# A hybrid attention backbone on one core: the second layer's gate products placed between its attention steps

## The chip, the core and the metric

The kernel runs on one core of one Trainium2 chip, as one program. The metric is device time in microseconds (us). Before the change the median of three runs is 2137.03 us (2135.74 to 2137.96).

The core has a matrix engine (TensorE, PE), a vector engine (VectorE, DVE), a scalar engine (ScalarE, ACT), a general engine (GpSimd, POOL) and a queue that issues most transfers (SyncE, SP). Each takes its own instructions in the order in which the program lists them; semaphores hold an instruction back until what it needs is there. So an instruction that waits also holds all that stands behind it on its engine.

## The reference

Two layers work on 256 latent tokens x and 256 context tokens h, 1024 channels each. Cut to what matters here:

```python
for l in range(DEPTH):                       # DEPTH = 2
    x, h = x + ffn(...), h + ffn(...)        # half-step SwiGLU
    # mixing: u = modulated norm; one input projection gives all of these
    cq, ckv, kr, dq, dk, dv, pool_in, gates = split(u @ w_in)
    o_mla  = softmax_attention(q(rmsnorm(cq)), k(rmsnorm(ckv), kr), v(...))   # 8 heads
    o_diff = (softmax(q1 k1) - lam * softmax(q2 k2)) @ dv                     # 8 heads, rms norm per head
    o_pool = pool_proj(window_mean(pool_in) - pool_in)                        # 4 groups, windows 2/4/8/16
    g = sigmoid(gates + b_gate)                                               # 3 branches x 1024 channels
    merged = g[0]*(o_mla @ w_br_mla) + g[1]*(o_diff @ w_br_diff) + g[2]*(o_pool @ w_br_pool)
    x = x + mod * (merged @ w_out)           # h likewise, not in the last layer
    x = x + ffn(...)                         # h likewise, not in the last layer
return rmsnorm(x)
```

In the second layer only x is needed after the mixing, so queries, gates, branches and the output work on 256 columns, and only keys and values on all 512.

## The kernel before

**Products.** Activations lie as 128 channels by 512 tokens (latent in columns 0 to 255). Every product is done as three passes on fp32r data: high part times high part, and the two cross products with a low part (`mm3`, L305; the matmul itself is L310). A weight block of 128x128 against 256 tokens is thus three matmuls, and a product over 1024 input channels is 24.

**Weights.** They stream from memory as 406 chunks of 128x1024 float32 (512 KB), in the order in which the products ask for them (`Weights.take`). When a product opens chunk c, `pump` requests chunk c+3: SP loads it (`w`, L152), ACT casts its high part (`hi`, L153), and the low part (`lo`, L161) is a subtraction, on POOL in two halves of 128x512 while `on_pool` is true, otherwise on DVE in one 128x1024 instruction. There are four raw buffers and four of each part. The first 24 chunks of the second layer's mixing (271 to 294) were split earlier and lie in memory as two parts, so SP loads both and no engine works on them.

**Mixing.** It has 12 attention units in the second layer: eight of differential attention (0 to 7: four head pairs, two query blocks each), then four pairs of heads of latent attention (8 to 11). A unit is a score product into PSUM banks (L820, or L1148), a softmax (row maximum on DVE, exponential on ACT, L836 or L1170), norm steps (POOL and DVE; L1179 in the latent units), a transposition on PE (`tr`, L883) that ACT and DVE split into `pth` and `ptl`, and the product with the values (`po`, L906 to L909).

**The order between units** is written out by hand. SCHEDULE has one string for each layer, cut at `|` into rounds. Round 0 stands before the first unit, round n behind the scores and softmax of unit n-1, and rounds 13 to 18 in the merge below. A token is an item issued at that point: `dk1` to `dk3` and `dq1` to `dq3` the differential keys and queries, `kv`, `cq`, `kr` the latent inputs, `ls` their norms' statistics (its `rb` is the broadcast, L968, behind a reciprocal, L945), `k`, `q`, `v0`/`v1`, `ma` to `md` further keys, queries and values, `p0` to `p3` a pool group's product with its POOL work, `pp` the split of that (`pdh`, L349), `pj` its projection, `st`/`dn` the head norms, `om` the split of a latent output. `N` is the next norm step of the last unit, `T` the transposition of the oldest open unit, `V` its value product, `P` and `D` put `on_pool` to true and false.

**Gates.** `g<dm><b>` is one of the 24 gate products (output block dm 0 to 7, branch b: 0 latent, 1 differential, 2 pool), 24 matmuls each. One that stands in a round up to 12 is copied out of PSUM (L1303), written to memory (L1308) and fetched back (L1315) in the merge; one in round 13 or later is copied and stays in its page. Those that no round names are made in the merge loop, with the sigmoid straight from PSUM (L1396); the others take the sigmoid from their page (L1391).

**Merge.** For each dm, in the order b = 2, 1, 0: the gate (made or taken), then the branch product `br` (12 matmuls), then gate times branch on DVE (L1407). In dm = 0 a round is issued behind each gate and each branch. At dm = 1 `on_pool` becomes false.

Of the kernel before, what the change touches and what calls it, by code (L numbers as in the profile page):

```python
# [17 lines left out]
D = 1024  # L18
KD = 8
T = 512  # L20
# [35 lines left out]
)  # L56


# [1748 lines left out]
```

## Time and profile before

| | |
|---|---|
| median of three runs | 2137.03 us (2135.74 to 2137.96) |
| the profiled execution | 2135.98 us, span 2134.2 us |
| mean granted clock of PE | 0.997 |
| PE busy | 2110.2 us, 99% of the span |
| DVE, ACT, POOL busy | 61%, 42%, 41% |
| transfers | 409.21 MB, mean 192 GB/s |

The span is what the trace covers; the time of the execution has 1.8 us around it. Times in the rows are microseconds from the span's start. The second layer's attention lies at about 1640 to 1830, its merge at about 1830 to 1900.

### The profile page before, as it was taken

To read this page: it belongs to the slowest core of one execution; us is meant where nothing else is said; L and a number is where in the kernel's file an instruction comes from. 1 tells how busy PE (TensorE), PEld (TensorE's weight loads), DVE (VectorE), ACT (ScalarE), POOL (GpSimd) and SP (SyncE) were. 2 spreads that over 40 slices of the span, in tenths; PEclk is the share of its full clock that TensorE was granted. 3 is DMA by queue.
4 is the path that set the end of the run, shared out by engine and by line. 5 is a ranking of instruction groups with operands and counts; after the bars stand their busy time and mean duration, and the time that the engine had idled before them with its cause. 6 is when DMAs were issued, how large, how long until landed. Compare 5 with 4: busy or idle time off the path is not lost.

```text
span 2134.2 us, 31733 instructions
## 1 busy us (share of the span) xinstructions
PE 2110.2 (99%) x12068; PEld 1821.0 (85%) x12068; DVE 1297.5 (61%) x2008; ACT 899.4 (42%) x1530; POOL 883.5 (41%) x768
## 2 busy tenths in 40 slices
PE   9999999999999999999999999999999999999998
PEld 6888888977887788988888898888889888999998
DVE  7565655456656799457647644443444777567755
ACT  4433233345565533432212243332333557555544
POOL 0443435322475411567657754444353347401000
PEclk9999999999999999999999999999999999999999
DMA  7477777354322466245444526776674642455653
GB/s 286 178 295 278 252 265 281 106 207 138 114 94 74 150 235 237 99 158 180 167 166 162 178 95 226 286 286 237 250 263 153 225 163 99 166 198 192 232 182 116
DMA packets 119533, 409.21 MB, mean 192 GB/s; under 512 B 13266, under 2 KB 17234, under 8 KB 119380
## 3 DMA queue, kind: packets, MB, share of 16 engines
q1 hardware_dynamic: 103540, 354.74, 47.4%
q10 hardware_dynamic: 15840, 52.44, 6.2%
q8 instruction: 95, 1.56, 0.3%
q14 instruction: 58, 0.48, 0.1%
HBM read 348.80 MB, written 58.33 MB: 191 GB/s over the span
## 4 chain that ended last, share of the span: by engine, by line
PE 90%; ACT 4%; DVE 4%; issue 1%; POOL 1%; DMA 0%; ACTq 0%; DVEq 0%; POOLq 0%
PE dn L310 22%; PE fg L310 19%; PE fu L310 19%; PE gt L310 8%; PE it L310 7%; PE br L310 5%; PE vi L310 2%; ACT pe L836 1%; PE fg L1614 1%; PE fu L1614 1%; PE tr L883 1%; PE pa L1541 1%; PE sc L1148 1%; PE po L907 1%; ACT pe L1170 1%
## 5 line engine op out<-in xcount | busy, mean ns | idle before, releaser
L161 POOL TENSOR_TENSOR lo<-w,hi 128x512 fp32r<-128x512 f32 x410 | 644.7, 1597 | 583.2 <-ACT hi L153 552.7
L153 ACT CAST hi<-w 128x1024 fp32r<-128x1024 f32 x359 | 375.0, 1048 | 586.2 <-DMA w<-in_stream 227.6
L280 DVE CUSTOM_DVE_ANT_0 junk<-a,cvec 128x1024 bf16<-128x1024 f32 x224 | 350.6, 1565 | 3.7
L161 DVE TENSOR_TENSOR lo<-w,hi 128x1024 fp32r<-128x1024 f32 x154 | 188.8, 1232 | 139.7 <-ACT hi L153 139.6
L310 PE MATMUL dn<-hh,hi 128*128 128x512 f32 (+1 forms) x800 | 272.7, 341 | 0.0
L310 PE MATMUL dn<-hl,hi 128*128 128x512 f32 (+1 forms) x800 | 272.2, 340 | 0.0
L310 PE MATMUL dn<-hh,lo 128*128 128x512 f32 (+1 forms) x800 | 272.2, 340 | 0.0
L310 PE MATMUL fg<-uh,hi 128*128 128x512 f32 (+2 forms) x712 | 252.1, 354 | 0.0
L310 PE MATMUL fg<-ul,hi 128*128 128x512 f32 (+2 forms) x712 | 251.6, 353 | 0.0
L310 PE MATMUL fu<-ul,hi 128*128 128x512 f32 (+2 forms) x712 | 251.6, 353 | 0.0
L310 PE MATMUL fu<-uh,hi 128*128 128x512 f32 (+2 forms) x712 | 251.6, 353 | 0.0
L310 PE MATMUL fg<-uh,lo 128*128 128x512 f32 (+2 forms) x712 | 251.5, 353 | 0.0
L310 PE MATMUL fu<-uh,lo 128*128 128x512 f32 (+2 forms) x712 | 251.5, 353 | 0.0
L310 PEld LDWEIGHTS dn<-hl,hi 128*128 128x128 f32 x800 | 151.7, 190 | 17.0
L310 PEld LDWEIGHTS dn<-hh,hi 128*128 128x128 f32 x800 | 151.7, 190 | 17.0
L310 PEld LDWEIGHTS dn<-hh,lo 128*128 128x128 f32 x800 | 151.7, 190 | 16.7
L610 DVE TENSOR_TENSOR h<-sg,fu 128x512 f32<-128x512 f32 x66 | 45.2, 686 | 189.0 <-PE fu L310 110.8
L649 DVE SCALAR_TENSOR_TENSOR X<-dn,md,X 128x256 f32<-128x256 f32 x112 | 50.1, 479 | 173.0 <-PE dn L310 173.0
L310 PEld LDWEIGHTS fu<-uh,lo 128*128 128x128 f32 x712 | 134.5, 189 | 18.4
L310 PEld LDWEIGHTS fg<-ul,hi 128*128 128x128 f32 x712 | 134.6, 189 | 18.4
L310 PEld LDWEIGHTS fu<-uh,hi 128*128 128x128 f32 x712 | 134.6, 189 | 18.4
L310 PEld LDWEIGHTS fg<-uh,lo 128*128 128x128 f32 x712 | 134.5, 189 | 18.4
(322 smaller groups left out, 4367.4 us busy)
## 6 DMA issues: line engine op xcount, KB each, us to landing
w<-in_stream SPq DMA_DIRECT2D x359, 512.0 KB, 4.2
a<-in_ada SPq DMA_DIRECT2D x136, 512.0 KB, 4.6
el<-in_stream SPq DMA_DIRECT2D x47, 512.0 KB, 3.6
early<-eh ACTq DMA_DIRECT2D x47, 512.0 KB, 2.7
early<-el ACTq DMA_DIRECT2D x47, 512.0 KB, 3.7
hi<-early SPq DMA_DIRECT2D x47, 512.0 KB, 4.3
lo<-early SPq DMA_DIRECT2D x47, 512.0 KB, 5.3
a<-in_stream SPq DMA_DIRECT2D x8, 512.0 KB, 5.0
```

The lines of the kernel that those rows point to most:

```text
L153: copy(hi, raw)
L161: eng.tensor_tensor(out=lo[:, c], in0=raw[:, c], in1=hi[:, c].bitcast(F32), op=ALU.subtract)
L280: nc.vector.tensor_tensor_reduce(out=self.junk, in0=raw, in1=self.cvec[:, s, :], scale=1.0, scalar=0.0, op0=ALU.mult, op1=ALU.add, accum_o ...
L310: nc.tensor.matmul(out, a, b, start=first and n == 0, stop=last and n == 2)
L610: nc.vector.tensor_tensor(out=h[:, c], in0=sg[:, c], in1=pu[:, c], op=ALU.mult)
L649: nc.vector.scalar_tensor_tensor(out=x, in0=p[:, SC[s]], scalar=K.mod(self.l, m, s, dm), in1=x, op0=ALU.mult, op1=ALU.add)
L836: nc.scalar.activation(e[:, c], banks[i][:, c], AF.Exp, bias=nm[:, o:o + 1], scale=1.0, accum_out=ls[:, o:o + 1])
L883: nc.tensor.transpose(t[:, i * 128:i * 128 + 128], P[:, i * 128:i * 128 + 128], self.ident)
L907: nc.tensor.matmul(out[0:64], v[:, o:o + 64], lo[:, n, :], start=False, stop=False)
L1148: nc.tensor.matmul(out[qt], a[0:96, q0:q0 + 128], b[0:96, kc], start=n == 0, stop=n == 2)
L1170: nc.scalar.activation(e[:, o:o + nk], out[qt], AF.Exp, bias=nm[:, i:i + 1], scale=1.0, accum_out=ls[:, i:i + 1])
L1614: nc.tensor.matmul(b, w[n // 2], x, start=k == n == 0, stop=k == KD - 1 and n == 2)
```

## The change

Only the second string of SCHEDULE is another one. No instruction's shape changes and PE has the same matmuls.

```diff
-    "dk1 dq2 N | N P N N N dq1 cq0 kv0 | P N T kv1 N | N N | dk2 N N N N D N N dk3 N N T N N dq3 cq1 N N N V N "
-    "cq2 P N N N | N V g10 N N N N | N T N N ls T v0 nk0 nk1 V N kr N kc0 N nq0 kc1 nq1 | nq2 N v1 N N V P N kc2 "
-    "N | kc3 g20 N P T q1 V T N k0 q4 q0 q2 g41 T N V p3 V N k1 ma N | mb q3 T q5 k2 | N V sq T N p1 | g50 st N "
-    "ds1 V N mc N pp1 md N N N N N q6 N T N N q7 k3 pp3 N N pj1 p2 g12 | N T N ds0 N V om0 N pp2 | V dr1 N dn3 "
-    "p0 g11 dr0 dn1 om1 pj2 T pj3 N pp0 g00 om2 pj0 dn0 V | dn2 g01 N | | om3 N | N |",
+    "N dq3 N N dq1 | kv0 | dk1 N cq0 N dq2 N N N | T P N N V N P N N N D N dk2 N kv1 | P N T N dk3 N N N g40 N "
+    "cq1 N | N N T N cq2 N V N N N N | N N g10 ls v0 T V nk0 nk1 N kr N N N kc0 nq0 kc1 N nq1 P | nq2 N v1 N g20 "
+    "P N kc2 T N | kc3 V q1 N V q4 T q2 q0 k0 g31 T N N V p3 | ma T N k1 N g41 N k2 q3 q5 V mb g32 | | g02 N N V "
+    "sq N T N p1 g50 N st N V mc pp1 N md N N g71 N q6 T q7 k3 p2 pp3 N V ds1 pj1 N N ds0 g22 | N pp2 N | g51 "
+    "om0 g42 T g60 g12 dr1 dr0 g11 om1 p0 pj3 g72 pj2 V dn3 dn0 T N g52 pp0 g00 g70 pj0 g01 g61 g30 dn1 | g62 "
+    "dn2 V om2 | om3 N | N | N N N N N |",
```

Before, five gates are spilled (g10, g20, g41, g50, g12), three are made in rounds 13 and 14 and kept, and 16 are left to the merge loop. Now ten are spilled (g40, g10, g20, g31, g41, g32, g02, g50, g71, g22), 13 are kept from rounds 13 and 14, and one, g21, is left to the loop. So five more gates stand ahead of the last unit, and ten more stand behind it in the first rounds of the merge. Counted over the program, 14 chunks' low parts move from DVE to POOL (410 to 438 halves on POOL, 154 to 140 on DVE), SP gets five more spills and five more fetches of 128 KB, ACT 15 more copies, and 15 sigmoids read a page instead of PSUM.

The first place is the ACT engine around unit 9, the second pair of latent heads. `qf<-it` is the copy of a query product out of PSUM, `qh` the cast of a finished query, `kh` a key, `mv` a value, `pe,ls<-sc,nm` the exponentials of a unit. Before:

```order
L1170 ACTIVATE pe,ls<-sc,nm 128x512 x4
L349 CAST mv<-vi 128x4x64 x2
L153 CAST hi_15772<-w_15774 128x1024
L1109 COPY qf<-it 64x256
L349 CAST pth<-tr 128x4x128 x2
L1109 COPY qf<-it 64x256
L352 ACTIVATE qh_15794<-qf 96x256
L349 CAST kh<-it 64x512 x2
L352 ACTIVATE qh_15826<-qf 96x256
L1170 ACTIVATE pe,ls<-sc,nm 128x512 x4
```

And now:

```order
L1171 ACTIVATE pe,ls<-sc,nm 128x512 x4
L350 CAST mv<-vi 128x4x64 x2
L350 CAST pth<-tr 128x4x128 x2
L350 CAST kh<-it 64x512 x2
L1304 COPY sg<-gt 128x256
L350 CAST kh<-it 64x512 x2
L1110 COPY qf<-it 64x256 x2
L353 ACTIVATE qh_15864<-qf 96x256
L350 CAST mv<-vi 128x4x64 x2
L154 CAST hi_15905<-w_15907 128x1024
L154 CAST hi_15912<-w_15914 128x1024
L353 ACTIVATE qh_15882<-qf 96x256
```

The two query copies now stand next to each other, behind a gate's copy and a second pair of keys, and values and weight casts stand between the finished queries. Behind this piece the exponentials of units 9 and 10 follow each other.

The second place is the POOL engine, where the last pool group's work (`pp`, `pw`, `po`, `ed`) stands among the weights' low parts. Before:

```order
L161 TENSOR_TENSOR lo_16316<-w_16317,hi_16315 128x512 x2
L1179 TENSOR_SCALAR pe<-pe,ri 128x512 x4
L161 TENSOR_TENSOR lo_16457<-w_16458,hi_16456 128x512 x2
L161 TENSOR_TENSOR lo_16521<-w_16522,hi_16520 128x512 x2
L1021 MEMSET pp 128x8
L1022 MEMSET pp 128x8
L1031 TENSOR_TENSOR pw<-pp 128x271
L1038 TENSOR_SCALAR po_16542<-pw 128x256
L1040 TENSOR_TENSOR po_16542<-po_16542,pp 128x256
```

And now:

```order
L162 TENSOR_TENSOR lo_16519<-w_16520,hi_16518 128x512 x2
L1180 TENSOR_SCALAR pe<-pe,ri 128x512 x4
L162 TENSOR_TENSOR lo_16602<-w_16603,hi_16601 128x512 x2
L162 TENSOR_TENSOR lo_16640<-w_16641,hi_16639 128x512 x2
L162 TENSOR_TENSOR lo_16706<-w_16707,hi_16705 128x512 x2
L162 TENSOR_TENSOR lo_16740<-w_16741,hi_16739 128x512 x2
L162 TENSOR_TENSOR lo_16778<-w_16779,hi_16777 128x512 x2
L162 TENSOR_TENSOR lo_16816<-w_16817,hi_16815 128x512 x2
L1022 MEMSET pp 128x8
L1023 MEMSET pp 128x8
L1032 TENSOR_TENSOR pw<-pp 128x271
L1039 TENSOR_SCALAR po_16837<-pw 128x256
```

Between the last unit's norm (`pe<-pe,ri`) and the last pool group stood the low parts of two chunks, now those of six.

The third place is ACT where that pool group is split (`pdh<-po`) for its projection `pj0`. Before:

```order
L349 CAST pth<-tr 128x4x128 x4
L349 CAST oph_16649<-pf 128x256
L349 CAST pdh<-po_16542 128x256
L153 CAST hi_16661<-w_16663 128x1024
L1303 COPY sg<-gt 128x256
L349 CAST omh_16691<-om_14335 128x256
L349 CAST oph_16701<-pf 128x256
```

And now:

```order
L350 CAST pth<-tr 128x4x128 x4
L154 CAST hi_16974<-w_16976 128x1024
L1304 COPY sg<-gt 128x256
L350 CAST pdh<-po_16837 128x256
L154 CAST hi_17012<-w_17014 128x1024
L1304 COPY sg<-gt 128x256
L154 CAST hi_17046<-w_17048 128x1024
L1304 COPY sg<-gt 128x256
L350 CAST oph_17082<-pf 128x256
```

A gate's copy now stands ahead of the split and two behind it before the projection's result (`oph`), where only one stood behind it.

## Rows read from the trace of the kernel before

**Rows 1.** Windows: stretch, length; busy PE, PEld, DVE, ACT, POOL; PEclk, DMA share, GB/s

```profile
1600.00:1700.00 100.00, 98.28 (x729) 89.50 (x729) 56.79 (x123) 42.21 (x101) 33.72 (x41) 1.00 0.55 190
1700.00:1800.00 100.00, 94.02 (x666) 82.54 (x665) 73.52 (x132) 63.11 (x145) 50.83 (x69) 0.98 0.36 123
1800.00:1830.00 30.00, 27.64 (x199) 25.19 (x198) 19.53 (x34) 20.73 (x44) 24.66 (x34) 0.94 0.49 163
...
1870.00:1910.00 40.00, 40.00 (x335) 40.00 (x335) 24.62 (x34) 20.50 (x31) 3.01 (x4) 1.00 0.61 203
```

**Rows 2.** Waits of PE, 1500 to 1960: total us, times, longest us

```profile
PE sc L1148 <- ACT qh L352: 3.8, 1, 3.8
PE it L310 <- ACT pdh L349: 2.1, 1, 2.1
PE rb L968 <- DVE r L945: 1.4, 1, 1.4
PE it L310 <- ACT pe L836: 1.3, 1, 1.3
PE it L310 <- ACT pe L1170: 0.7, 1, 0.7
PE it L310 <- DMA lo<-early: 0.3, 1, 0.3
```

**Rows 3.** Timeline of PE at unit 9: start, us, instruction [idle before <- releaser]

```profile
1754.47 0.28 PE L310 MATMUL it<-cqh,lo 128*128 128x256 f32 x1
...
1760.29 0.39 PE L1148 MATMUL sc<-kh,ql 96*128 96x512 f32 x1
1764.46 0.69 PE L1148 MATMUL sc<-kh,qh 96*128 96x512 f32 x1 [3.77 <-ACT qh L352]
```

**Rows 4.** Timeline of ACT at the same place

```profile
1760.49 0.36 ACT L1109 COPY qf<-it 64x256 f32<-64x256 f32 x1
...
1763.99 0.42 ACT L352 ACTIVATE qh<-qf 96x256 fp32r<-96x256 f32 x1 [1.90 <-POOL qf L1113]
```

**Rows 5.** Timeline of DVE ahead of the broadcast of the latent norms

```profile
1706.92 3.34 DVE L945 RECIPROCAL r<-r 2x512 f32<-2x512 f32 x1
```

**Rows 6.** Timeline of PE at the last pool group's projection

```profile
1819.39 0.28 PE L310 MATMUL gt<-uh,hi 128*128 128x256 f32 x1
...
1822.15 0.28 PE L310 MATMUL gt<-uh,lo 128*128 128x256 f32 x1
1824.53 0.39 PE L310 MATMUL it<-pdh,hi 128*128 128x256 f32 x1 [2.09 <-ACT pdh L349]
```

**Rows 7.** Timeline of POOL at the last pool group

```profile
1813.02 5.22 POOL L161 TENSOR_TENSOR lo<-w,hi 128x512 fp32r<-128x512 f32 x4
...
1820.82 0.19 POOL L1048 TENSOR_TENSOR po<-ed,pp 128x1 f32<-128x1 f32 x1
```

**Rows 8.** Line L161 in 1735 to 1850: duration ns min/median/max, first and last start

```profile
L161 POOL TENSOR_TENSOR lo<-w,hi x30: 1262/1293/1502, 1750.9 to 1838.8; 128x512 fp32r<-128x512 f32 x30
```

**Rows 9.** The page, part 5: groups of the whole program (busy us, mean ns | idle before)

```profile
L161 POOL TENSOR_TENSOR lo<-w,hi 128x512 fp32r<-128x512 f32 x410 | 644.7, 1597 | 583.2 <-ACT hi L153 552.7
L153 ACT CAST hi<-w 128x1024 fp32r<-128x1024 f32 x359 | 375.0, 1048 | 586.2 <-DMA w<-in_stream 227.6
...
L161 DVE TENSOR_TENSOR lo<-w,hi 128x1024 fp32r<-128x1024 f32 x154 | 188.8, 1232 | 139.7 <-ACT hi L153 139.6
```

**Rows 10.** Transfers issued in 1735 to 1850: KB each, median us to landing

```profile
w<-in_stream SPq DMA_DIRECT2D x22, 512.0 KB, 3.9
...
sg<-g SPq DMA_DIRECT2D x4, 128.0 KB, 2.2
```

**Rows 11.** Lines by form, 1735 to 1850: busy us, mean ns | idle before

```profile
L1179 POOL TENSOR_SCALAR pe<-pe,ri 128x512 f32<-128x512 f32 x16 | 11.1, 716 | 5.6 <-DVE ri L1177 4.0 <-PE vi L310 1.6
...
L1407 DVE TENSOR_TENSOR sg<-sg,br 128x256 f32<-128x256 f32 x7 | 2.8, 412 | 0.3 <-ACT sg L1391 0.3
...
L1391 ACT ACTIVATE sg<-sg,vec 128x256 f32<-128x256 f32 x6 | 2.9, 502 | 0.0
```

## The prediction

> **What bounds the kernel now.** I read the busy shares first: PE is busy 99% of the span, so only PE's idle time and its clock can be won. Next the windows, to find where PE loses anything [rows 1]. From 1600 to 1700 it lacks 1.72 us, from 1700 to 1800 it lacks 5.98, from 1800 to 1830 it lacks 2.36, and from 1870 to 1910 nothing: 10.06 us, all in the second layer's attention, none in its merge. The granted clock is below 1 in the same two stretches: 0.98 over 100 us and 0.94 over 30 us, so about 2.0 and 1.8 us more went at 1.2 instead of 2.4 GHz; I count 3.5. The ceiling of what the change can win is thus 13.6 us.
>
> Then PE's waits, which name six causes [rows 2]: the second query of unit 9 (3.8), the last pool group's split (2.1), the latent norms' broadcast (1.4), PSUM banks not yet read by exponentials (1.3 and 0.7), and a weight part still on its way (0.3), together 9.6. The timelines of these places show why each is late [rows 3 to 7]. The clock fell behind the 3.8 and the 2.1 only; the waits of 1.4, 1.3 and 0.7 lie in the same two stretches or the one before and left no mark of that size.
>
> **The change part by part.** PE gets the same matmuls, so its own work adds nothing. A gate is 24 of them at 0.12 us (23 steps from 1819.39 to 1822.15 [rows 6]), 2.88 us, and can be laid into any of these holes. What counts is whether the chains are done behind the new covers.
>
> *Unit 9's query* (3.8 us and a clock fall of 1.7). The query's product ended at 1754.6, its copy on ACT ran only at 1760.49, and the cast came 3.5 us later, at 1763.99, behind a turn on POOL [rows 3, 4]. The second head's scores were wanted at 1760.5, 5.9 us after the product. Now q3 is followed by q5 (9 matmuls, 1.1 us), mb (12, 1.4), g32 (24, 2.9) and the first head's scores (six of 512 columns at twice the price, 1.4): 6.8 us. Unit 8's exponentials, which kept ACT from the copy, start earlier, since k1 and g41 stand between that unit and q3. With the copy within 2 us, plus 0.36 and 3.5, the cast is ready a microsecond ahead. I take 0 left. If the copy is as late as before, 5.9 us behind, then 5.9 + 3.9 − 6.8 = 3.0 us and the clock's 1.7 stay.
>
> *The last pool group* (2.1 and 1.7). POOL came to it at about 1818.2, behind four halves of weights, and finished at 1821.0 [rows 7]; the projection wanted it at 1822.3 and got it at 1824.53, since ACT's and DVE's work on the transposition stood ahead of the split [rows 6]. Now six chunks stand ahead of it on POOL, but between p0 and pj0 stand pj3, g72, pj2, a value product, a transposition and three more gates: four gates alone are 11.5 us. POOL's own item is 2.8 us, one chunk ahead of it 2.6. I take 0 left; at worst the 3.8 stay.
>
> *Banks.* Units 2 and 3 followed each other and cost 1.3; now cq0, dq2 and norms stand between them. Units 9 and 10 now follow each other instead. Their eight banks are free if unit 8's exponentials are done by then, and g32 gives them 2.9 us: 0, or again 1.3.
>
> *Latent norms* (1.4). The chain through the root and the 3.34 us reciprocal [rows 5] has the same cover as before, v0 and a transposition; g10 stands now ahead of the statistics and helps nothing behind them. I leave 1.0, between 0 and 3.
>
> *Start.* dq3, dq1 and kv0 now open the mixing, and their split weights arrive while the transfers are crowded; the 0.3 may stay. *Latent output.* om3's split has less work in front of its branch: 0.3, at most 2.
>
> *Weights in the tail.* Fourteen chunks' low parts move from DVE to POOL. A chunk is two halves of 1.293, 2.59 us [rows 8], against 2.88 for a gate that eats one. From request to need lie three chunks of gates, 8.64 us; the load takes 3.9, the cast 1.05, the low part 2.59, together 7.5 [rows 8 to 10]. One microsecond is left, less where a small item opens a chunk; I put 0.5 there. The latent norms on POOL (four of 0.72, 2.9 us [rows 11]) and the pool item 2.8 lie where chunks are ahead.
>
> *Spills.* Five more copies on ACT and five more transfers of 128 KB each way stand on SP between weight loads that are ordered three chunks ahead; cost 0 in the attention. A spill waits on SP for its gate's copy, and the next weight load behind it, for under 1 us of the one that is left. The 24 sigmoids and the products with the branches stay; 15 more of the sigmoids read a page, at 0.50 us each on ACT [rows 11], in a merge that has no gate products beside them any more (the first rival).
>
> For holes that I don't see I add one of the typical size, 1.4. Sum: −13.6 + 1.0 + 0.3 + 0.3 + 0.5 + 1.4 = −10.1 us on the profiled execution of 2135.98 (its span 2134.2 and 1.8 around it), so 2125.9. That execution lies 1.05 below the median of the runs: 2127.
>
> **The rivals.**
>
> *Slower: the merge becomes a chain through late gates.* Before, 16 gates lay between the branches and PE lost nothing there. Now a block is three branches, 36 matmuls, 4.3 us. Its spilled gates are fetched one block ahead: the fetch stands on SP behind weight loads that wait for a raw buffer (up to 2.9), takes 2.2 [rows 10], and the sigmoid 0.5: 5.6 against 4.3. DVE, in order, would stand at the product of gate and branch with the next chunk's low part behind it (1.23 of DVE, [rows 9]), and PE would wait for that. At 1.3 to 2.9 us in each of six blocks that is 8 to 17; 12.5 and a clock fall make 2141. It decides once a fetch and its sigmoid need over 4.3 us. For it: DVE's load, per block 1.5 × 1.23 + 3 × 0.41 + about 0.5 of sums, 3.6 of 4.3 us. Against it: DVE was busy 24.6 of 40 there, transfers moved at 0.61 [rows 1], and eight PSUM banks let PE run ahead. A mild form only at the end, where the last splits have no gates as cover, costs 5 and a clock fall: 2133.
>
> *POOL binds the tail.* POOL's halves are 1293 ns in this stretch but 1597 on average over the program [rows 8, 9]. At 1597 a chunk is 3.19, 0.31 over a gate; over some 20 chunks 6.2, less the stretches without gates: 3 to 6, plus a clock fall: 2132 to 2134. The Trainium skill speaks for this (SBUF — State Buffer, section SBUF: two separate sides): a GpSimd instruction that reads SBUF and a VectorE one with two SBUF inputs share a port pair, and the later one stands still for the whole of the other. In the stretch the longest half is 1502 [rows 8], 0.2 above the median, so the trace shows little of it here.
>
> *The holes come back.* ACT's order around unit 9 still puts the query's turn behind casts, and the pool group stands behind more chunks: 3.8 + 1.7 + 1.3 + 2.1 + 1.7 = 10.6 stay, and the time is 2137, no change. Against it stand the longer covers.
>
> **How the numbers follow.** Forecast as summed 0.57 (its own range 2123.4, the whole ceiling won, to 2131); mild end of the merge 0.11; chain through the merge 0.08; POOL 0.10; holes back 0.14. About 0.2%, 4.3 us, is what a measurement of this kernel can tell from no change: faster is below 2132.8, slower above 2141.3. Faster: 0.57 + 0.06 + 0.05 + 0.02 = 0.70. Same: 0.05 + 0.05 + 0.11 + 0.01 = 0.22. Slower, the chain and a little of the holes with new ones: 0.08. The range runs from 2122 to 2138: little can lie below the ceiling, and above lies most of the chain.
>
> **What would show it.** Right: PE lacks under 5 us between 1600 and 1830, the waits on `qh` and `pdh` are gone, the granted clock of all stretches to 1900 is 1.00, the wait of `rb` is about 1. Wrong: PE waits for `lo` or for sums in the merge, DVE idle there for `sg` from a transfer, POOL's halves above 1.45 us in the tail, or a clock fall at a new place.

## The result, and the profile after

The changed kernel takes 2125.3 us (median of four runs, 2123.84 to 2127.01) against 2137.43 in the runs beside it: ratio 0.9945, 95% interval 0.9928 to 0.9962, so 8 to 15 us less. The forecast was 2127, its range 2122 to 2138. The execution that was profiled is the fastest of the four, 2123.84 us.

All but 1.2 us of it lies where it was looked for. Two marks stand in the same place of both programs: the first product of the mixing behind the feed-forward, and the first product with the output weights behind the merge. In the kernel before (timeline of PE: start, us, instruction):

```profile
1618.46 0.28 PE L310 MATMUL it<-uh,hi 128*128 128x256 f32 x1
...
1911.11 0.28 PE L310 MATMUL dn<-mh,hi 128*128 128x256 f32 x1
```

And in the changed one:

```profile
1617.22 0.28 PE L311 MATMUL it<-uh,hi 128*128 128x256 f32 x1
...
1898.86 0.28 PE L311 MATMUL dn<-mh,hi 128*128 128x256 f32 x1
```

292.65 us became 281.64: a gain of 11.0 us, of which 0.3 went back right behind the second mark (a wait for the last split). The 1.24 us ahead of the first mark arose in the first layer, where both programs have the same order; I take it for the spread between two executions.

The windows of the changed kernel, same columns as [rows 1]:

```profile
1600.00:1700.00 100.00, 99.44 (x740) 90.55 (x739) 58.02 (x125) 42.72 (x102) 31.11 (x39) 1.00 0.60 202
1700.00:1800.00 100.00, 97.67 (x714) 86.40 (x713) 69.47 (x119) 64.67 (x144) 60.30 (x76) 1.00 0.40 134
1800.00:1830.00 30.00, 30.00 (x243) 29.51 (x242) 14.74 (x24) 22.37 (x44) 26.07 (x31) 1.00 0.53 185
1830.00:1860.00 30.00, 30.00 (x243) 28.88 (x241) 12.23 (x18) 16.34 (x28) 28.19 (x27) 1.00 0.47 159
1860.00:1900.00 40.00, 39.97 (x329) 39.42 (x329) 28.77 (x52) 26.09 (x47) 11.68 (x13) 1.00 0.70 238
```

PE lacks 0.56 + 2.33 = 2.9 us up to 1830 where it lacked 10.06, and the granted clock is 1.00 throughout where two stretches of 3.4 us had run at half. So 7.2 us of idle time and 3.4 us of clock make 10.6, the 10.7 that the mixing gained. POOL is busy 28.2 of 30 us from 1830 to 1860, and PE does not wait there at all.

PE's waits now (1500 to 1950; total us, times, longest us), against [rows 2]:

```profile
PE it L311 <- ACT pp L1024: 1.3, 1, 1.3
PE tr L884 <- DVE od L918: 0.5, 1, 0.5
PE gt L311 <- DVE ptl L351: 0.4, 1, 0.4
PE sc L1149 <- ACT qh L353: 0.4, 1, 0.4
PE tr L884 <- ACT pe L837: 0.2, 1, 0.2
```

None of the six old waits is left in its place; the 0.4 us on `qh` is at 1746.23, ahead of unit 8 and not of unit 9. The largest new wait, 1.3 us, is at `k1`. What made it stands in three timelines. SP's queue first (the issue of a gate's spill, then of a weight load):

```profile
1747.54 0.32 SPq L1309 DMA_DIRECT2D g<-sg  x1
1747.91 1.37 SPq L153 DMA_DIRECT2D w<-in_stream  x1
```

Then ACT and PE:

```profile
1747.14 0.37 ACT L1304 COPY sg<-gt 128x256 f32<-128x256 f32 x1
...
1752.33 1.04 ACT L154 CAST hi<-w 128x1024 fp32r<-128x1024 f32 x1 [3.23 <-DMA w<-in_stream]
1753.40 0.37 ACT L1024 COPY pp<-it 128x256 f32<-128x256 f32 x1
```

```profile
1753.82 0.50 PE L311 MATMUL it<-ckvh,hi 128*128 128x512 f32 x1 [1.28 <-ACT pp L1024]
```

The spill of g31 waited on SP for the gate's copy at 1747.14; the weight load behind it was issued only then, landed 4.3 us later, and ACT stood 3.23 us at the cast of that chunk. Behind the cast on ACT stands the copy that frees a PSUM bank, and PE's product needs that bank. No engine of this chain is short of time; what delays PE is the order in SP's queue.

### The profile page after: what moved, and what is told of

Read it like the earlier page. It is cut to its first block, busy times and chain, and to the rows that moved or that the text cites. A ratio compares the mean times of both kernels' runs of the same rounds, so it can differ in the third digit from the quotient of the medians.

```text
span 2122.0 us, 31778 instructions
## 1 busy us (share of the span) xinstructions
PE 2105.3 (99%) x12068; PEld 1817.7 (86%) x12068; DVE 1283.0 (60%) x1994; ACT 904.2 (43%) x1545; POOL 919.8 (43%) x796
## 4 chain that ended last, share of the span: by engine, by line
PE 94%; ACT 3%; DVE 2%; issue 1%; DMA 0%; POOL 0%; DVEq 0%; ACTq 0%; SPq 0%; POOLq 0%
PE dn L311 23%; PE fg L311 19%; PE fu L311 19%; PE gt L311 9%; PE it L311 8%; PE br L311 4%; PE vi L311 3%; PE tr L884 1%; PE sc L1149 1%; PE fg L1615 1%; PE fu L1615 1%; PE sc L821 1%; PE po L908 1%; ACT pe L837 1%; PE pa L1542 1%
## 5 line engine op out<-in xcount | busy, mean ns | idle before, releaser
L162 POOL TENSOR_TENSOR lo<-w,hi 128x512 fp32r<-128x512 f32 x438 | 680.9, 1579 | 578.8 <-ACT hi L154 574.5
L162 DVE TENSOR_TENSOR lo<-w,hi 128x1024 fp32r<-128x1024 f32 x140 | 171.0, 1230 | 115.9 <-ACT hi L154 115.7
L381 POOL TENSOR_TENSOR acc<-acc,sq 128x256 f32<-128x256 f32 (+1 forms) x49 | 45.5, 928 | 247.7 <-ACT sq L377 247.3
```

Source lines behind the costliest of these rows:

```text
L162: eng.tensor_tensor(out=lo[:, c], in0=raw[:, c], in1=hi[:, c].bitcast(F32), op=ALU.subtract)
L381: eng.tensor_tensor(out=self.acc[:, cols], in0=self.acc[:, cols], in1=sq[:, cols], op=ALU.add)
```

## The experiments

Intervals are those of the ratio to the kernel before, which ran beside each. The first theory: each hole is a chain that lacks cover, and giving it cover is the whole gain. Rivals: the gain comes from having gates out of the merge, or from moving the low parts to POOL.

**One gate behind q3, in the kernel before.**

```diff
- mb q3 T q5 k2
+ mb q3 g32 T q5 k2
```

> The kernel before with one token added: a gate (g32) behind q3, ahead of unit 9's scores; one gate less in the merge. Theory (each hole is a chain that lacks cover, and the clock falls only behind the long ones): the 3.8 us wait on qh shrinks to 1.0 or less, the half-clock stretch behind it is gone, so about -2.9 to -3.8 and -1.7: 2132 to 2133 against 2137.4. Rival (the gain of the change comes from fewer gates in the merge or from the low parts on POOL): one gate of 24 moves, so 0 to -0.5. Rival (the query's chain is in order behind the gate's copy on ACT and shifts with it): the wait stays at 3 us or more, 0 to -1.

Ratio 0.9997 (0.9987 to 1.0006): nothing that can be measured, and at most 2.8 us less, where 4.6 or more had been forecast. Its waits and the window behind unit 9:

```profile
PE it L310 <- ACT pdh L349: 2.1, 1, 2.1
PE sc L1148 <- ACT qh L352: 1.6, 1, 1.6
PE rb L968 <- DVE r L945: 1.4, 1, 1.4
PE it L310 <- DMA lo<-early: 1.3, 1, 1.3
...
PE sc L1148 <- DVE ql L353: 0.5, 1, 0.5
```

```profile
1764.00:1772.00 8.00, 7.48 (x31) 6.37 (x31) 7.21 (x13) 3.92 (x11) 5.01 (x7) 0.57 0.25 97
```

The wait fell from 3.8 to 2.1 (1.6 and 0.5), not to 1.0. By the timeline of ACT the copy of the query, at 1759.79, still ran only behind unit 8's exponentials and a weight's cast. And the clock fell all the same, for 6.8 us instead of 3.4 (0.57 on average over 8 us). In this execution the clock thus took back the 1.7 us that half filling the hole had won. The time alone doesn't separate the theory from the rival, which had 0 to -0.5; the wait that shrank does.

**One gate ahead of pj0, in the kernel before.**

```diff
- pp0 g00 om2 pj0 dn0 V | dn2 g01 N
+ pp0 g00 om2 g01 pj0 dn0 V | dn2 N
```

> The kernel before with g01 moved from round 14 to stand ahead of pj0 in round 13. Theory: the wait on pdh (2.1 us) is gone with the half-clock stretch behind it, -3.8: about 2133.6. Rival (the wait comes from POOL, loaded with low parts, and moves to the next item): the wait stays or turns up at om3 or at a low part, 0 to -1.

0.9982 (0.9973 to 0.9992), 3.8 us less (1.7 to 5.8): the theory's size. The profiled execution is the slowest of its ten (2135.94 us; the clock was at half for 6.8 us at each of two other places in it), so the wait is read from it and not the time. In the stretch of the merge's first rounds, where 2.1 stood, PE waits now for

```profile
PE br L310 <- DVE odl L350: 0.4, 1, 0.4
PE br L310 <- ACT odh L349: 0.2, 1, 0.2
```

**Both.**

> Both edits: a gate behind q3 and a gate ahead of pj0. Theory: the two add, -7 to -8.5: 2129 to 2130.4, two thirds of the whole change by two tokens; no half-clock stretch before the end of the program. Rivals: as for each, together 0 to -2.

0.9983 (0.9974 to 0.9993), no more than the second alone. The wait on `qh` was 2.8 us in its profile: ACT had waited 2.0 us for a weight load ahead of it. The two do not add: two tokens are worth 3.6 us (1.5 to 5.6) of the change's 11.8, about a third and not two thirds.

**T behind v0, in the kernel before.**

```diff
- ls T v0
+ ls v0 T
```

> The kernel before with T moved behind v0 in round 6, as the changed kernel has it. The forecast left 1.0 us of the wait for the broadcast of the latent norms, and the changed kernel has none. Theory: the transposition's casts (pth, 1.1 us on ACT) stood ahead of the root's table load in before; behind v0 they stand behind it, and the transposition itself now lies between v0 and the broadcast: the wait of 1.4 falls to under 0.3. Rival (it vanished because of another unit order or DVE work): the wait stays over 1.0.

2134.87 us in a single run, and `PE rb L968 <- DVE r L945: 1.4, 1, 1.4`: the wait stayed, and the theory fell. The casts in front of the root's table load are those of another transposition, the first `T` of that round, which the edit does not move and which the changed order does not have there.

**Cover taken away from the changed kernel, at unit 9.**

```diff
- V mb g32 | | g02
+ V mb | | g32 g02
```

> The changed kernel with g32 moved from between q3 and unit 9 to behind unit 10. Theory: unit 9's second head is wanted 2.9 us earlier, at 1764.5, and its query's parts are ready at 1766.5: a wait of about 2 us returns; if it is 2.1 or more the clock falls behind it for 3.4 us at half (1.7): +2 to +3.7 against the changed kernel, 2127.3 to 2129. Rival (the gain comes from fewer gates in the merge, which are as many here): 0.

0.9973 (0.9963 to 0.9982): 2131.21, some 6 us above the changed kernel, more than forecast, and not for the forecast reason. Unit 9 lost next to nothing: its query came 0.15 us late, and the two waits on `qh` below, at 1747.67 and 1772.01, are those of units 8 and 10. The wait at `k1` was longer, and a new hole opened at `st`:

```profile
PE st L992 <- ACT hi L154: 3.0, 1, 3.0
PE it L311 <- ACT pp L1024: 1.9, 1, 1.9
PE sc L1149 <- ACT qh L353: 0.9, 2, 0.5
```

SP and ACT ahead of it:

```profile
1781.10 0.33 SPq L1309 DMA_DIRECT2D g<-sg  x1
1781.52 0.38 SPq L153 DMA_DIRECT2D w<-in_stream  x1
```

```profile
1785.40 1.05 ACT L154 CAST hi<-w 128x1024 fp32r<-128x1024 f32 x1 [4.33 <-DMA w<-in_stream]
```

g32's copy now stands on ACT behind the exponentials of two units, its spill waits on SP for it, and the weight load behind the spill is late: the chain of `k1` again, and this time 3.0 us. The clock was at half for 6.8 us from 1791.3 on, a microsecond before that wait ended, and for 3.4 us behind the 1.9 at `k1`:

```profile
1791.00:1799.00 8.00, 6.69 (x26) 4.12 (x27) 3.50 (x4) 6.19 (x9) 6.99 (x15) 0.57 0.46 173
```

This execution, 2134.75 us, is one of the two slowest of ten (2128.25 to 2134.8), so a typical one lost less than its holes add up to.

**Cover taken away at the last pool group.**

```diff
- g52 pp0 g00 g70 pj0
+ g52 pp0 pj0 g00 g70
```

> The changed kernel with pj0 moved ahead of g00 and g70. Theory: the split of the last pool group ended about 3.1 us before it was wanted; wanted 5.8 us earlier, it is 2.7 us late: a wait of 2 to 3 us and a half-clock stretch (1.7), +3.5 to +4.5. Rival as above: 0.

0.9970 (0.9959 to 0.9982): 2131.62, about 6 us above the changed kernel. The wait is the forecast one, the fall twice as long (0.57 over 8 us, 3.4 us of loss instead of 1.7):

```profile
PE it L311 <- ACT pdh L350: 2.7, 1, 2.7
...
PE it L311 <- DVE pdl L351: 0.5, 1, 0.5
```

```profile
1841.00:1849.00 8.00, 6.68 (x31) 6.38 (x32) 2.26 (x4) 2.25 (x6) 5.20 (x4) 0.57 0.19 66
```

**Five gates given back to the merge.**

```diff
- | g51 om0 g42 T g60 g12 ... g01 g61 g30 dn1 | g62 dn2
+ | g51 om0 T g12 ... g01 dn1 | dn2
```

> The changed kernel with five gates that cover no wait (g42, g60, g61, g30, g62) given back to the merge loop. Theory (only cover counts): 0, within 1 us, PE's waits as in the changed kernel; the pool group has less ahead of it, 3 us of spare cover hold. Rival (gates ahead of the merge are themselves worth something, 10.7 us for 15 gates): +3.5.

0.9938 (0.9923 to 0.9953), 2124.76: not above the changed kernel, where the rival had +3.5. Gates that cover nothing have no worth that these runs can tell. In its profile the wait at `k1` is 1.8 us, and the clock is at half for 3.4 us behind it, which it was not in the changed kernel's.

**Low parts of the tail on DVE.**

```diff
- | g51 om0 g42
+ | D g51 om0 g42
```

> The changed kernel with the low parts of round 13's weights on DVE instead of POOL. Theory: POOL is not what PE waits for, 0 within 1 us. Rival (POOL's load binds the tail, or the two engines block each other): a gain of 1 us or more. The other rival (taking the low parts off DVE is what the change gains by): +3 or more.

0.9937 (0.9921 to 0.9954), 2124.22: no difference either way that these runs can tell. Sixteen chunks' low parts went back to DVE here (406 halves on POOL, against 438 in the changed kernel and 410 in the kernel before). So POOL at 94% was not what PE waited for, and neither is moving work to it what the change gains by.

**Second theory: a spill on SP holds the weight loads.** The spill is issued from ACT's queue, right behind the copy.

```diff
-            nc.sync.dma_start(d[:, c], t[:, c])
+            (nc.sync if both else nc.scalar).dma_start(d[:, c], t[:, c])
```

> The changed kernel with the second layer's gates spilled from ACT's queue instead of SP's (one word). Theory, new after the runs so far: a spill stands on SP until its gate's copy has run on ACT, and the weight load behind it is late; in the changed kernel that made the 1.3 us wait of k1's product (its PSUM bank is freed by a copy that stands behind a weight's cast, which waited 3.2 us for its load). Without it that wait is gone and ACT's 3.2 us for a load too: -1 to -2 against the changed kernel, 2123 to 2124. Rival (the bank is late for ACT's exponentials, not for the load): the wait stays within 0.3, time 0. Rival (issuing on ACT costs its order): +0.5 to +2.

0.9935 (0.9923 to 0.9948), 2124.04. The wait at `k1` is gone, and ACT no longer waits for that chunk; unit 10's query (0.6 us, at 1768.85) is a little late in its place; the other 0.4 on `qh` is unit 8's, as in the changed kernel:

```profile
PE sc L1149 <- ACT qh L353: 1.0, 2, 0.6
PE gt L311 <- DVE ptl L351: 0.5, 1, 0.5
PE gt L311 <- ACT pe L1171: 0.3, 1, 0.3
```

The mechanism is shown by the wait that went; the 1.3 us below the changed kernel are less than the intervals can separate.

**The same with g32 behind unit 10.**

> The kernel with g32 behind unit 10, again with spills from ACT's queue. There PE waited 3.0 us at st: g32's copy stood behind two units' exponentials, its spill was issued at 1781.1, the load behind it landed at 1785.4, and ACT waited 4.3 us for it. Theory: that wait falls under 1 us and the half-clock stretch behind it goes, -3 to -6 against the kernel with spills on SP: 2126 to 2128. Rival (g32's place itself costs, as first forecast): the 3.0 stay, 2131.

0.9952 (0.9938 to 0.9965), 2127.75; with spills on SP the same order had 0.9973. The 3.0 at `st` and the wait at `k1` are gone, and what the first theory had forecast for g32's place is now to be seen:

```profile
1764.26 0.39 PE L1149 MATMUL sc<-kh,ql 96*128 96x512 f32 x1
1766.98 0.50 PE L1149 MATMUL sc<-kh,qh 96*128 96x512 f32 x1 [2.33 <-ACT qh L353]
```

```profile
1768.00:1776.00 8.00, 8.00 (x41) 6.88 (x41) 4.64 (x11) 5.80 (x13) 6.24 (x6) 0.79 0.23 72
```

The wait is 2.3 us (2.0 had been worked out), and the clock costs 1.7. The time is 3.7 us above the kernel that differs in g32's place alone, with no run of either in the other's range. So g32 is the cover of unit 9, as forecast; with spills on SP that had been hidden, since with the late load at `k1` PE came to unit 9 later itself.

**All three** (spills from ACT, five gates back, low parts on DVE).

> The changed kernel with spills from ACT, the five gates given back to the merge, and the low parts of round 13 on DVE: the best guess from the runs so far. Each of the last two was within 1 us of the changed kernel. Theory: 2122 to 2124. Rival (margins add up against it at the merge's end, where a wait of 0.3 us was seen with the five gates back): 2125 or more.

0.9942 (0.9929 to 0.9956), 2125.2: no better than the changed kernel, and outside the 2122 to 2124 that the theory had; the rival had 2125 or more. Its profile has two waits of 0.2 us for the last splits behind the merge, which do not make up the difference to the kernel with spills from ACT alone; the rest is within the spread. No version beat the changed kernel beyond the intervals.

**Spills from ACT in the kernel before.**

> The kernel before with its five spills from ACT's queue. Theory: the waits on qh (3.8) and pdh (2.1) were not made by late loads; they stay within 0.5 us. Rival (the spills on SP made the holes of the kernel before as well): one of the two falls under 1 us.

2134.91 us in a single run; the waits on `qh` (3.8) and `pdh` (1.9) stay. The holes of the kernel before were lack of cover, not late loads.

## Why the prediction was right

*Ceiling and sum.* The 13.6 us at hand and the 3.5 left over (forecast) stand against 2.9 left over and none of the clock lost. By the marks the mixing gained 10.7, forecast 10.1. That the two left-overs are so close is in part luck. Of the 3.5, 2.1 stood for the norms, the start, the latent output and the tail's weights, and PE has no such wait up to the second mark. Of the 2.8 us of waits that it has instead, the sum knew 1.4, for holes that I did not see. And that no clock was lost holds for the fastest of the four executions, with a mean granted clock of 0.999; the other three had 0.998.

*What is shown of the gain.* Unit 9's cover is worth 3.7 us by the two kernels with spills from ACT, the last pool group's 3.8 by the gate ahead of pj0. The rest, some 4 us, is read from waits that are gone (the norms', the banks', the start's); no run isolates these.

*Unit 9.* Right. The copies began at 1762.89 and the cast ran from 1765.41 to 1765.83, the second head was wanted at 1767.43: 1.6 us ahead, where 1 was forecast. The copy began 2.2 us behind its product and not within 2, but the cast followed 2.5 us after the copy's start and not 3.5; and the copy's 0.36 had been counted twice, since the 3.5 ran from its start already.

```profile
1762.89 0.64 ACT L1110 COPY qf<-it 64x256 f32<-64x256 f32 x2
1765.41 0.42 ACT L353 ACTIVATE qh<-qf 96x256 fp32r<-96x256 f32 x1 [1.89 <-POOL qf L1114]
```

That g32 is what covers it is shown by the kernel with spills from ACT: 2.3 us without it.

*The last pool group.* Right. POOL worked off six chunks without a pause and the group behind them, done at 1837.9. ACT came to the split 4 us later, behind the transposition's casts, a weight's cast and a gate's copy; its half ended at 1842.4 and DVE's at 1843.4. The product was due at 1845.7:

```profile
1819.58 15.62 POOL L162 TENSOR_TENSOR lo<-w,hi 128x512 fp32r<-128x512 f32 x12
...
1837.72 0.19 POOL L1049 TENSOR_TENSOR po<-ed,pp 128x1 f32<-128x1 f32 x1
```

Taking 5.8 us of cover away brought back a wait of 2.7, the one worked out, and cost some 6 us with what the clock added.

*Latent norms.* Wrong by the 1.0 us that I left: the chain was seen as unchanged. In the changed kernel ACT comes to the root without the casts of an earlier transposition, and the reciprocal ends at 1709.15 where PE asks at 1709.35; before, it ended at 1710.3 where PE had asked at 1708.9 [rows 2, 5]:

```profile
1705.82 3.33 DVE L946 RECIPROCAL r<-r 2x512 f32<-2x512 f32 x1
```

On ACT, in the kernel before and in the changed one, what stands ahead of the root's table load:

```profile
1703.63 1.08 ACT L349 CAST pth<-tr 128x512 fp32r<-128x512 f32 x2
1704.73 1.28 ACT L358 ACT_TABLE_LOAD   x1
```

```profile
1702.87 0.38 ACT L1304 COPY sg<-gt 128x256 f32<-128x256 f32 x1
1703.27 1.28 ACT L359 ACT_TABLE_LOAD   x1
```

That these casts are the cause is read from the timelines only; the run that was to test it moved the wrong transposition.

*Spills.* The step that was mis-sized: "A spill waits on SP for its gate's copy, and the next weight load behind it, for under 1 us". The load was 3.2 us late for ACT and PE lost 1.3; in the order with g32 late it was 4.3 and 3.0. The sum held only since 1.4 had been set aside for unseen holes, and since nothing came of the terms named above. By the Trainium skill's account (Perfetto Trace Analysis, section Per-instruction lifecycle: what the profiler-reported window actually captures) ACT, DVE and GpSimd take their queue strictly in order; the chain above agrees, 3.23 us of ACT idle with a ready copy behind.

*Rivals.* The merge did not become a chain: DVE waited for no fetch there, though three of the ten fetches took 5.8 to 6.5 us to land, longer than the 4.3 of cover that I gave them. SP issues them further ahead than I took: the two gates of dm = 4 were fetched from 1872.05 on and landed by 1878.3, and PE came to that block at 1881.6. Nor did POOL bind: with DVE in its place the time was the same. Its halves were as short as before:

```profile
L162 POOL TENSOR_TENSOR lo<-w,hi x56: 1262/1291/1498, 1747.2 to 1861.2; 128x512 fp32r<-128x512 f32 x56
```

The average of 1597 over the program [rows 9] comes from elsewhere. In the kernel before, 133 of the 410 halves took over 1.7 us, and 110 of these overlap DVE's reduction of line 280, which reads two operands from SBUF; of the 277 shorter ones 34 do. So the rule of the Trainium skill that was cited ahead (SBUF — State Buffer, section SBUF: two separate sides) shows in this trace. The reduction does not run in the tail. Short instructions of DVE with two operands in SBUF do, the low parts of splits, and beside POOL's halves it is they that stand still: 0.57 to 1.50 us each for 128x256 in the changed kernel, against 0.42 alone. POOL's halves there take at most 1.50. The last pool group's own split is one of those that stood still, with 1.05.

## What to carry to other kernels

Price a hole of PE by what follows it too: half a hole filled may win nothing (the first experiment), and only the chain's own end, worked out against the new time at which it is wanted, tells if it is filled. An instruction that waits on a queue is paid by what stands behind it: a small store that waits for a late copy does not belong in the queue that feeds the weights. Work moved for cover is worth its place and nothing else: five of fifteen moved gates could go back without a cost that could be measured.

## What the hardware showed that was not expected

The clock's fall does not go by the length of the wait alone. A wait of 1.4 us for the latent norms left it at full speed in the kernel before, and in the kernel with a gate ahead of pj0 the same wait was followed by 6.8 us at half:

```profile
1709.00:1717.00 8.00, 7.69 (x18) 3.62 (x19) 4.95 (x9) 2.10 (x4) 0.00 (x0) 0.57 0.00 0
```

The 2.1 us wait for `pdh` was followed by a fall in the kernel before and by none in the kernel with a gate behind q3, at the same place of the program:

```profile
1824.00:1834.00 10.00, 7.62 (x50) 6.08 (x49) 6.70 (x15) 5.18 (x11) 5.25 (x5) 1.00 0.40 132
```

The clearest case is in the first layer: at about 510 to 513 us every one of the fourteen traces has the same three waits of 0.24 to 0.36 us. In one of them, that of the kernel with g32 late and spills from ACT, the clock was at half behind them, for 3.4 us from 512.6 on (0.79 on average over 511 to 519); in the other thirteen it was not.

A fall within the layers lasted 3.4 or 6.8 us, so a hole of 1.4 to 3 us cost nothing, up to 1.7 or up to 3.4 us more. What decides between these no run here tells. So the 1.7 us that the prediction set behind each of two holes are sizes seen in one execution, and the condition set for g32's late place, a fall from a wait of 2.1 us on, does not hold: 2.13 us went without one and 1.8 us did not. It fits that the kernel before, with its holes, ranged from 2135.1 to 2140.2 in the 15 runs beside the second four experiments, and the kernel with spills from ACT, almost without holes, from 2123.7 to 2125.0 in five; that the holes make this spread is argued, not shown.
